# The stores of 48 gate blocks to DRAM, issued by GpSimd instead of ScalarE, in a hybrid decoder trunk

## The chip, the core and the metric

The program runs on one core of one Trainium2 chip. The metric is device time in microseconds (us) of one execution; smaller is better. The engines are named as the profile names them: PE (TensorE), PEld (its weight load), DVE (VectorE), ACT (ScalarE), POOL (GpSimd) and SP (SyncE). ACTq, SPq and POOLq are the instruction queues of these engines where DMAs are issued from them.

## The reference, cut to what matters

Two residual layers (DEPTH 2) on a sequence of 512 rows with 1024 channels, in float32. Each layer projects the normalized input with one matrix, and its columns feed three branches and three blocks of gate logits. The three branch outputs are projected, each is multiplied by the sigmoid of its gate logits, and the sum goes through an output matrix; a gated MLP with a short convolution follows.

```python
h = rmsnorm(x, norm1_g[l])
p = h @ w_in[l]
p_rw, p_ret, p_sg, gate_logits = jnp.split(p, in_cuts, axis=-1)
...
branches = jnp.stack([y_rw, y_ret, y_sg], axis=2)
proj = jnp.einsum('bsgc,gcd->bsgd', branches, w_branch[l])
gates = jax.nn.sigmoid(gate_logits.reshape(B, S, N_BRANCH, D_MODEL))
x = x + jnp.sum(gates * proj, axis=2) @ w_out[l]
x = x + conv_ffn(rmsnorm(x, norm2_g[l]), ffn_w_up[l], ffn_conv_w[l], ffn_conv_b[l], ffn_w_down[l])
```

The gate logits are 3 x 1024 channels, which the kernel holds as 24 blocks of 128 channels by 512 rows for each layer, 48 in all.

## The kernel before, in words

**Matrix products.** Every weight block `wr` comes from DRAM by SP (L136). ACT rounds it to the format fp32r (`wh` or `sh`, L176), DVE subtracts to get the rest (`wl` or `sl`, L181), and PE multiplies in three passes (L198: high by low, high by high, low by high). A weight block is cast two to five blocks ahead of its use. The buffers `wh` and `wl` are three deep, so a cast waits until PE is done with the block three back.

**The gate blocks.** `gates` (L556) is a generator of filler work. While the RWKV branch does its many small and dependent steps, the program takes one step after another from the generator, so that PE always has large matrix products to do. For each of the 24 blocks of a layer PE fills `acc`, DVE multiplies it by the row norm into the tile `gth` (L566), ACT applies tanh in place (L567), and the tile is stored to a block `gd` in DRAM (L569). Much later, in the merge, POOL's queue loads the block back (L1167).

**What else stands on these queues in that stretch.** On ACT: casts of weight blocks, copies `Y`, `GB`, `bk`, `zs`, and in the recurrence (from about 200 us) the copies `U` (L825) and `y` (L842), which PE or DVE then needs. On POOL: masks by affine select (L702, L703), copies of `cs` and `GB` (L899), loads `bkS` (L744), loads of MLP weights `cs` (L337), the small power `rs` for the group norm (L857), loads `yF` (L280), `tab` (L995), and stores `ts` (L308). On SP: weight loads `wr`, the transposing round trips `tr`, `Vt`, `bkS` through DRAM.

**What sets the order.** A scheduler with a timeline of its own puts the instructions of each engine in order when the program is built; each engine then runs its list in that order. Some instructions are pinned to the order in which the code names them. The program also gives each DMA one of a few counters: DMAHW0 to DMAHW7 go round among the DMAs of SP's and ACT's queues, DMASW0 to DMASW7 among those of POOL's queue. A DMA that takes a counter first waits until the DMA before it on that counter has landed. This is seen in the listing with waits, below.

Of the kernel before, what the change touches and what calls it, by code (L numbers as in the profile page):

```python
# [54 lines left out]
class Emit:  # L55
# [500 lines left out]
    def gates(self, l):  # L556
        self.gd = {}
        for br in range(3):
            for m in range(8):
                pg = self.acc()  # L560
                g = self.matFg(pg, ("wall", l, 34 + br * 8 + m, 0), self.h)
                next(g)
                yield
                next(g)
                t = self.u(n="gth")
                self.nc.vector.tensor_tensor(t, pg, self.rsF, op=MUL)  # L566
                self.nc.scalar.activation(t, t, AF.Tanh, scale=0.5)  # L567
                d = self.dp.tile([128, 512], F32, name=self.nm("gd"))
                self.nc.scalar.dma_start(d, t)  # L569
                self.gd[br, m] = d  # L570
                yield

# [1188 lines left out]
```

## Time and profile before

| | us |
|---|---|
| median of 3 runs | 1682.23 (1681.42 to 1682.3) |
| the profiled execution | 1682.15 |
| its span in the profile | 1680.2 |
| PE busy in the span | 1670.6 (99%) |
| DVE busy | 1289.4 (77%) |
| ACT busy | 820.8 (49%) |
| POOL busy | 333.3 (20%) |

The profiled execution is 1.95 us longer than its span, and 0.08 us from the median. The granted TensorE clock is 0.999 over the span. In the timeline a row has the start in us, the duration in us, the engine, the line, the operation with the tile that it writes and what it reads, the count, and in brackets the idle time of the engine before it with what ended it. Rows marked ACTq or SPq are DMA issues, which are not counted as busy; DMA issues of POOL are counted as POOL's work.

### The profile page before, as it was taken

How to read it: one execution, taken by the hardware profiler on the slowest of the kernel's cores; microseconds unless marked ns; L12 is line 12 of the kernel's file. 1: busy time of each engine (PE TensorE's matmuls, PEld its weight loads, DVE VectorE, ACT ScalarE, POOL GpSimd, SP SyncE). 2: the span in 40 equal slices, each digit the busy share in tenths (PEclk: the TensorE clock that was granted, in tenths of full speed). 3: DMA queues.
4: the chain of work that ended last, by engine and by line, in shares of the span. 5: the costliest groups of instructions: out<-in, count | busy, mean ns of one | idle time of the engine just before them, and what ended most of it. 6: DMA issues, size and time to landing. Idle time of an engine off the chain costs nothing.

```text
span 1680.2 us, 29344 instructions
## 1 busy us (share of the span) xinstructions
PE 1670.6 (99%) x10643; PEld 1393.6 (83%) x10643; DVE 1289.4 (77%) x2289; ACT 820.8 (49%) x1436; POOL 333.3 (20%) x514
## 2 busy tenths in 40 slices
PE   9999999999999999999999999999999999999998
PEld 7888877888888888899988888778888888888887
DVE  7788746578668898977868887565785688888897
ACT  6564433554254444456655634435542544444565
POOL 1016013312210111100111260223122012221100
PEclk9999999999999999999999999999999999999999
DMA  5337555644553666668733375646444536665865
GB/s 184 94 102 236 166 180 166 191 129 129 179 191 110 212 216 224 211 226 297 236 111 95 106 227 159 210 155 189 124 141 150 157 128 205 210 203 176 277 232 174
DMA packets 155521, 298.39 MB, mean 178 GB/s; under 512 B 21936, under 2 KB 28848, under 8 KB 155376
## 3 DMA queue, kind: packets, MB, share of 16 engines
q1 hardware_dynamic: 123744, 215.02, 39.9%
q0 software_dynamic: 23280, 66.35, 12.0%
q10 hardware_dynamic: 8352, 15.15, 2.5%
q8 instruction: 83, 1.36, 0.3%
q14 instruction: 62, 0.51, 0.1%
HBM read 236.40 MB, written 60.03 MB: 176 GB/s over the span
## 4 chain that ended last, share of the span: by engine, by line
PE 99%; DVE 1%; DMA 0%; ACT 0%; issue 0%; DVEq 0%; ACTq 0%
PE acc L198 87%; PE sm L198 5%; PE sm L787 2%; PE sm L1044 1%; PE sm L694 1%; PE sm L1155 0%; PE acc L439 0%; PE sm L655 0%; PE sm L656 0%; PE sm L1102 0%; DMA wr<-wall 0%; PE sm L946 0%; PE acc L399 0%; PE sm L937 0%; PE sm L697 0%
## 5 line engine op out<-in xcount | busy, mean ns | idle before, releaser
L198 PE MATMUL acc<-lo,sh 128*128 128x512 f32 (+1 forms) x1144 | 442.6, 387 | 0.0
L198 PE MATMUL acc<-hi,sh 128*128 128x512 f32 (+1 forms) x1144 | 441.6, 386 | 0.0
L198 PE MATMUL acc<-hi,sl 128*128 128x512 f32 (+1 forms) x1144 | 429.3, 386 | 0.1
L176 ACT CAST sh<-wr 128x512 fp32r<-128x512 f32 x352 | 212.3, 616 | 215.3 <-PE acc L198 95.8
L176 ACT CAST wh<-wr 128x512 fp32r<-128x512 f32 x278 | 171.6, 619 | 282.3 <-PE acc L198 214.7
L181 DVE TENSOR_TENSOR wl<-wr,wh 128x512 fp32r<-128x512 f32 x278 | 196.3, 709 | 130.6 <-ACT wh L176 124.2
L181 DVE TENSOR_TENSOR sl<-wr,sh 128x512 fp32r<-128x512 f32 x352 | 238.8, 692 | 70.2 <-ACT sh L176 61.9
L198 PEld LDWEIGHTS acc<-hi,sl 128*128 128x128 f32 x1144 | 214.9, 188 | 44.1 <-DVE sl L181 0.5
L198 PEld LDWEIGHTS acc<-lo,sh 128*128 128x128 f32 x1144 | 215.0, 188 | 43.8 <-issue 0.5
L198 PEld LDWEIGHTS acc<-hi,sh 128*128 128x128 f32 x1144 | 215.0, 188 | 42.6
L198 PE MATMUL acc<-lo,wh 128*128 128x512 f32 (+1 forms) x636 | 244.6, 385 | 0.0
L198 PE MATMUL acc<-hi,wl 128*128 128x512 f32 (+1 forms) x636 | 242.7, 382 | 0.0
L198 PE MATMUL acc<-hi,wh 128*128 128x512 f32 (+1 forms) x636 | 242.4, 381 | 0.0
L1249 ACT ACTIVATE cv<-fu,pc 128x512 f32<-128x512 f32 x88 | 71.8, 816 | 170.1 <-DVE fu L1221 167.2
L198 PEld LDWEIGHTS acc<-hi,wl 128*128 128x128 f32 x636 | 119.6, 188 | 23.9 <-issue 0.7
L198 PEld LDWEIGHTS acc<-lo,wh 128*128 128x128 f32 x636 | 119.6, 188 | 23.3
L198 PEld LDWEIGHTS acc<-hi,wh 128*128 128x128 f32 x636 | 119.7, 188 | 22.3 <-issue 0.2
L1250 DVE SCALAR_TENSOR_TENSOR cv<-fu,pc,cv 128x511 f32<-128x511 f32 x88 | 65.9, 749 | 29.8 <-ACT cv L1249 29.5
L198 PE MATMUL acc<-wl,hi 128*128 128x512 f32 x212 | 85.8, 405 | 0.0
L198 PE MATMUL acc<-wh,lo 128*128 128x512 f32 x212 | 82.5, 389 | 0.0
L198 PE MATMUL acc<-wh,hi 128*128 128x512 f32 x212 | 82.4, 389 | 0.0
L308 POOL DMA_DIRECT2D ts<-pre x60 | 32.5, 542 | 192.1 <-DVE pre L163 184.2
(424 smaller groups left out, 2665.4 us busy)
## 6 DMA issues: line engine op xcount, KB each, us to landing
wr<-wall SPq DMA_DIRECT2D x480, 256.0 KB, 3.0
wr<-ts SPq DMA_DIRECT2D x76, 256.0 KB, 4.3
wr<-wdt SPq DMA_DIRECT2D x66, 256.0 KB, 3.6
pre<-wdt SPq DMA_DIRECT2D x60, 256.0 KB, 3.7
ts<-pre POOLq DMA_DIRECT2D x60, 256.0 KB, 2.7
gd<-gth ACTq DMA_DIRECT2D x48, 256.0 KB, 2.9
gth<-gd POOLq DMA_DIRECT2D x48, 256.0 KB, 3.5
sp<-ab SPq DMA_DIRECT2D x22, 256.0 KB, 5.3
```

The source lines that it names most:

```text
L176: self.at = [self.nc.scalar.copy(hi[:, :n], raw[:, :n])]
L181: self.at.append(self.nc.vector.tensor_tensor(lo[:, :n], raw[:, :n], hi[:, :n], op=SUB))
L198: i = self.nc.tensor.matmul(*x, **y, **kw)
L308: po(self.nc.gpsimd.dma_start(self.tsum[*q, p], t))
L694: i = T.matmul(pK[hv[1 - h], j, :], bk[hv[h], c, 1, :], x[hv[h], c, :], start=True, stop=True)
L787: po(T.matmul(o, l, r, start=start, stop=True, skip_group_check=True))
L1044: po(T.matmul(o, lhsT, rhs, start=start, stop=stop, skip_group_check=True))
L1249: self.nc.scalar.activation(t, u, AF.Identity, scale=self.p("cw2", j), bias=self.p("cb", j))
L1250: V.scalar_tensor_tensor(t[:, 1:], u[:, :511], self.p("cw1", j), t[:, 1:], op0=MUL, op1=ADD)
```

## The change

One word in `gates`: the store of a gate block is issued by `nc.gpsimd` instead of `nc.scalar`. The data, the sizes and all other lines are the same.

```diff
                 self.nc.scalar.activation(t, t, AF.Tanh, scale=0.5)
                 d = self.dp.tile([128, 512], F32, name=self.nm("gd"))
-                self.nc.scalar.dma_start(d, t)
+                self.nc.gpsimd.dma_start(d, t)
                 self.gd[br, m] = d
                 yield
```

The order on PE is the same, row for row. On ACT the 48 store rows are gone and nothing else moves. On POOL 48 rows are added and a few move past each other. On DVE and SP some neighbours swap places.

**ACT in the recurrence of layer 0**, where the copy `U` stands behind a store. Before, with what each row waits for in brackets (PE, DVE and Activation name engines, DMAHW a counter):

```order
L176 CAST wh_2561<-wr_2454 128x512 [waits DMAHW2_49,PE_49]
L176 CAST wh_2619<-wr_2497 128x512 [waits DMAHW4_49,PE_49]
L567 ACTIVATE gth_2577<-gth_2577 128x512 [waits DVE_49]
L569 DMA gd_2580<-gth_2577 128x512 [waits DMAHW2_49,Activation_49]
L825 COPY U_398<-sm_2541 128x256 [waits PE_49]
L176 CAST wh_2683<-wr_2559 128x512 [waits DMAHW5_49,PE_49]
```

Between the tanh of the gate block and the copy `U` stands a store that waits for counter DMAHW2. The change takes that row out, as the difference of the two lists shows:

```order
 L176 CAST wh_2561<-wr_2454 128x512
 L176 CAST wh_2619<-wr_2497 128x512
 L567 ACTIVATE gth_2577<-gth_2577 128x512
-L569 DMA gd_2580<-gth_2577 128x512
 L825 COPY U_398<-sm_2541 128x256
 L176 CAST wh_2683<-wr_2559 128x512
```

The copy `U` now follows the tanh directly.

**SP at the same place, before**, where the counter DMAHW2 was taken last:

```order
L744 DMA bkS_2516<-tr_2518 32x2x128 [waits DMAHW1_49]
L136 DMA wr_2617<-wall 128x512 [waits DMAHW2_49,DVE_49]
L744 DMA bkS_2516<-tr_2518 32x2x128 [waits DMAHW3_49]
L744 DMA bkS_2516<-tr_2518 32x2x128 [waits DMAHW4_49]
L744 DMA bkS_2516<-tr_2518 32x2x128 [waits DMAHW5_49]
```

The weight load `wr_2617` stands between the DMAs on counters 1 and 3; it holds counter 2 when the store on ACT asks for it.

**POOL in the recurrence of layer 0**, where stores now stand ahead of the loads `cs` and of the small power `rs`:

```order
+L569 DMA gd_2475<-gth_2472 128x512
+L569 DMA gd_2580<-gth_2577 128x512
 L337 DMA cs_2653<-wdt 128x512 x2
+L569 DMA gd_2702<-gth_2699 128x512
+L337 DMA cs_2654<-wdt 128x512 x2
 L857 TENSOR_TENSOR rs_522_2668<-s_521_2665,con 128x8
-L280 DMA yF_2671<-tr_2674 32x4x128 x4
-L337 DMA cs_2654<-wdt 128x512 x2
```

The loads `cs_2653` now stand behind the store of the gate block whose tanh precedes `U`; the loads `cs_2654` have moved from behind `yF` to ahead of `rs`, with one store ahead of them. The other layer has the same places.

## The prediction

> **What bounds the kernel now.** I read the page first: the busy shares and the chain that ended last.
>
> ```profile
> span 1680.2 us, 29344 instructions
> ...
> PE 1670.6 (99%) x10643; PEld 1393.6 (83%) x10643; DVE 1289.4 (77%) x2289; ACT 820.8 (49%) x1436; POOL 333.3 (20%) x514
> ...
> PE 99%; DVE 1%; DMA 0%; ACT 0%; issue 0%; DVEq 0%; ACTq 0%
> ```
>
> PE is busy for all but 9.6 us of the span, and the chain is PE from end to end. Its order is the same after the change. So a change on other queues can only take away, or add, time in which PE waits. Which such time there is stands in the list of PE's waits:
>
> ```profile
> PE acc L439 <- DVE rst L436: 1.5, 1, 1.5
> PE sm L787 <- ACT U L825: 1.0, 1, 1.0
> PE sm L787 <- DVE s L849: 0.4, 2, 0.2
> PE sm L694 <- issue: 0.3, 1, 0.3
> ```
>
> 3.2 us in five waits. One of them has to do with ACT, whose queue the change relieves: 1.0 us, once, for the copy `U`. I went to that place in the timeline, on PE, on ACT and on SP:
>
> ```profile
> 216.56 0.39 PE L198 MATMUL acc<-hi,wl 128*128 128x512 f32 x1
> 216.88 0.27 PE L787 MATMUL sm<-U,GB 64*64 64x64 f32 x1
> ...
> 224.97 0.22 PE L787 MATMUL sm<-XB,GB 64*64 64x64 f32 x1
> ...
> 227.72 0.39 PE L198 MATMUL acc<-hi,wl 128*128 128x512 f32 x1
> 229.10 0.27 PE L787 MATMUL sm<-U,GB 64*64 64x64 f32 x1 [0.99 <-ACT U L825]
> ...
> 224.86 0.63 ACT L567 ACTIVATE gth<-gth 128x512 f32<-128x512 f32 x1 [0.33 <-DVE gth L566]
> 228.28 0.35 ACTq L569 DMA_DIRECT2D gd<-gth  x1
> 228.67 0.37 ACT L825 COPY U<-sm 128x256 f32<-128x256 f32 x1 [3.19 <-DMA wr<-wall]
> ...
> 224.71 0.37 SPq L136 DMA_DIRECT2D wr<-wall  x1
> ```
>
> The tanh ends at 225.49, but the store behind it on ACT is issued only at 228.28: 2.79 us in which ACT stands still. The order shows why: the store wants the counter that a weight load of SP holds, and that load was issued at 224.71 and lands some 3.5 us later. `U` stands behind the store and runs at 228.67; PE comes to it right after the matmul at 227.72 and must wait. The same step a round earlier takes 0.32 us (216.56 to 216.88), here 1.38.
>
> **What the change removes.** The store leaves ACT, and `U` follows the tanh. It needs the products of PE that end at 225.19 (the L787 row at 224.97) and ACT, which is free from 225.49 on; its 0.37 us are done at about 225.9, well ahead of 227.72. The step on PE then falls to the 0.32 us of its neighbour: a gain of 1.38 - 0.32 = 1.06 us. Bounds: 0, if something else holds `U`, and 1.06.
>
> The other 47 stores leave ACT too. An issue takes 0.33 us of ACT's queue, 15.7 us for 48, and some wait much longer:
>
> ```profile
> L569 ACTq DMA_DIRECT2D gd<-gth x48: 326/327/369, 99.4 to 1078.5; - x48
> ...
> 210.11 0.63 ACT L567 ACTIVATE gth<-gth 128x512 f32<-128x512 f32 x1 [0.33 <-DVE gth L566]
> 214.22 0.37 ACTq L569 DMA_DIRECT2D gd<-gth  x1
> 214.69 0.62 ACT L176 CAST wh<-wr 128x512 fp32r<-128x512 f32 x1 [3.95 <-DMA bkS<-tr]
> ...
> 973.26 0.63 ACT L567 ACTIVATE gth<-gth 128x512 f32<-128x512 f32 x1 [0.33 <-DVE gth L566]
> 978.11 0.33 ACTq L569 DMA_DIRECT2D gd<-gth  x1
> 978.48 0.62 ACT L176 CAST wh<-wr 128x512 fp32r<-128x512 f32 x1 [4.58 <-DMA wr<-wall]
> ```
>
> Here ACT stood still for 3.48 us (210.74 to 214.22) and for 4.22 us (973.89 to 978.11), with a weight cast behind the store each time. PE's list has no wait for either: the weights are cast ahead, and that cover was longer than 4.2 us. So taking these away gives 0. This is the point at which the large figure, 10.5 us of stalls at three places alone, shrinks to 1.06.
>
> **What the change adds on POOL.** The nearest rows are the stores and loads that POOL issues already:
>
> ```profile
> ts<-pre POOLq DMA_DIRECT2D x60, 256.0 KB, 2.7
> gd<-gth ACTq DMA_DIRECT2D x48, 256.0 KB, 2.9
> ...
> L744 POOL DMA_DIRECT2D bkS<-tr x64: 533/533/728, 150.4 to 1003.7; - x64
> ...
> 159.40 8.50 POOL L744 DMA_DIRECT2D bkS<-tr  x16 [0.34 <-DVE TMP L916]
> ...
> 205.10 2.17 ACT L790 COPY bk<-bkS 128x512 f32<-128x512 f32 x4
> ...
> L1167 POOL DMA_DIRECT2D gth<-gd x48: 536/543/752, 361.7 to 1285.8; - x48
> ...
> 130.00:200.00 70.00, 70.00 (x431) 57.85 (x431) 58.79 (x120) 28.83 (x47) 27.39 (x43) 1.00 0.65 203
> ```
>
> A store of the same size from POOL (`ts`) lands in 2.7 us against 2.9 from ACT, and nobody reads `gd` before 361.7 us; the transfer itself is the same. An issue costs POOL about 0.54 us, bounds 0.53 and 0.75: 48 x 0.54 = 26 us on an engine that is busy for 333 of 1680. I take the middle row because these are DMAs of the same size. The last row is a stretch of 70 us in which most gates of layer 0 are stored (columns PE, PEld, DVE, ACT, POOL): POOL is busy for 27.4 of 70 and would go to about 35.
>
> What counts is who stands behind a store on POOL, since each store waits there for its tanh. The tightest places in layer 0:
>
> ```profile
> 190.60 0.63 ACT L567 ACTIVATE gth<-gth 128x512 f32<-128x512 f32 x1 [0.33 <-DVE gth L566]
> 193.32 2.40 POOL L899 COPY GB<-cs 32x1024 f32<-32x1024 f32 x2 [25.42 <-DVE cs L929]
> 195.67 1.14 POOL L337 DMA_DIRECT2D cs<-wdt  x2
> ...
> 233.61 0.62 ACT L567 ACTIVATE gth<-gth 128x512 f32<-128x512 f32 x1
> 235.22 1.68 POOL L857 TENSOR_TENSOR rs<-s,con 128x8 f32<-128x8 f32 x1 [38.42 <-DVE s L855]
> 236.94 0.69 DVE L859 TENSOR_TENSOR y<-y,rs 128x512 f32<-128x512 f32 x1 [1.87 <-POOL rs L857]
> ...
> 244.85 1.12 POOL L337 DMA_DIRECT2D cs<-wdt  x2
> 249.69 0.69 DVE L163 TENSOR_TENSOR cs<-cs,cs 128x512 f32<-128x512 f32 x1 [4.05 <-DMA cs<-wdt]
> ```
>
> - The copy `GB` (L899) has the store of the gate with the tanh at 190.60 ahead of it: that ends at 191.23, and the issue at 191.8, before 193.32. Cost 0.
> - The power `rs` (L857) now has a store and two `cs` loads ahead. The tanh ends at 234.23, then 3 x 0.54: POOL is free at 235.85 instead of 235.22. `rs` is 0.6 us late, and so is DVE's `y` (L859), on which DVE waits already for 1.87 us. Does PE feel it? The last row answers: DVE stood still for 4.05 us for the `cs` loads, with a weight difference `wl` queued behind, and PE's list has no wait there. 1.87 + 0.6 = 2.5 us stays under that. Cost 0.
> - The first `cs` pair goes from 195.67 to about 229, behind the stores; the second from 244.85 to about 235. Both are wanted by DVE from 245.6 on (249.69 - 4.05) and took about 4 us to come (245.4 to 249.69 for the second). At 239 they are there, and the 4.05 us wait on DVE goes. PE did not feel it, so the gain is 0.
> - The `bkS` loads of layer 0 (rows above) are issued from 150.4 to 167.9; two stores among them make that 1.1 us later, and their reader on ACT comes at 205.10. Cost 0.
>
> In layer 1 the same order meets the same spacing, and PE's list has no wait for `U` there, so there is nothing to gain.
>
> **The sum.** 1682.15 for the profiled execution, of which 1680.2 span and 1.95 around it, minus 1.06: 1681.09. The profiled execution lies 0.08 under the median, so the median after comes to 1681.2. What a measurement of this kernel can tell from no change is about 0.2%, 3.4 us: I forecast no change that shows.
>
> [...]
>
> **The rivals.**
>
> *The stall of `U` stays or comes back elsewhere.* The wait for `U` was a single one of 0.99 us; which round of the recurrence just misses is a matter of a microsecond, and SP's loads now take the counters in another order. Then 1682.2. For it: PE waits twice for DVE's `s` (0.2 us each) in the same stretch, so the margins there are small. Against it: nothing but the tanh is left between PE's products and `U`.
>
> *POOL is late with `rs`, and PE pays.* This ends on the other side. POOL takes its list in order, and a store or load ahead of `rs` that waits for a counter would hold `rs`. DVE waits for it in order, with the next `wl` behind it. It decides from the point at which DVE's wait passes the 4.05 us that were hidden: `rs` more than 2.2 us late (4.05 - 1.87). If a wait of a whole landing (5.7 us, the longest of the `gd` stores, in the row below) fell there, DVE would wait 1.87 + 0.6 + 5.7 = 8.2 us, PE would lose 4.1 in each layer, and the time would be 1681.2 + 8.2 = 1689.4.
>
> ```profile
> DMA to landing us min/median/max: 2.0/3.2/5.7
> ```
>
> Against it: each DMA on POOL waits for the one eight places earlier, and at this place that one is a gate store of the time before 200 us, more than 30 us back.
>
> [...]
>
> *ACT's freed time reaches PE.* If the three stalls were on the path after all, 10.5 us would go: 1671.7. Against it: PE's list has 1.0 us of waits for ACT in all.
>
> *The change does not do what it says.* The stores stand on POOL in the new order, all 48; only if POOL's waits came back to ACT through the `gth` tiles would nothing change. A tile comes round only after several other gate blocks. This falls together with the first rival: 1682.2.
>
> **How the numbers follow.** The forecast, the stall gone and nothing new: 0.68. The stall stays: 0.21. POOL late: 0.06. Locked out: 0.02. ACT's time reaches PE: 0.03. The first two are both within 0.2%: 0.89. Slower by over 0.2%: 0.08; faster: 0.03. The time is 1681.2. The range takes in both likely cases (1681.2 and 1682.2) with the spread of the three runs before (0.9 us) below, and above them 1.4 us for a small loss of the kind of the POOL rival: 1680.2 to 1683.6.
>
> **What would show it.** In the profile after: PE's list without the wait for `U`, and the step from the last matmul to L787 near 227 us at 0.32; the tanh of ACT followed at once by the next instruction, with the idle stretches of 2.8 to 4.2 us gone; no store on ACTq; POOL at about 360 us busy, its stores at 0.54 each; `rs` at about 235.9; the 4.05 us wait of DVE for `cs` gone. The prediction is wrong if PE's waits add up to more than 3.2 us, or if POOL's stores take over 1 us each, or if the time leaves the range with PE's waits unchanged.

## The result, and the profile after

The changed kernel takes 1684.22 us (median of 16 executions, 1682.27 to 1688.81) against 1681.81 before (16 executions on the same chip, 1681.19 to 1682.98). The ratio, which takes in all executions, is 1.0017, with a 95% interval of 1.0009 to 1.0025; by the two medians alone it would be 1.0014. So the change made the kernel 2.4 us slower by the medians, where the prediction had 1681.2 and a range up to 1683.6. A second comparison gave 1.0021 (1.0012 to 1.0030). Two of its twelve executions of the changed kernel, 2380.96 and 2793.79 us at a granted clock of 0.654 and 0.556, are left out of that ratio. The spread is part of the result: 1.8 us before, 6.5 us after.

The page of the changed kernel, its span, its busy times and its chain:

```profile
span 1682.9 us, 29386 instructions
...
PE 1671.8 (99%) x10643; PEld 1394.5 (83%) x10643; DVE 1291.1 (77%) x2289; ACT 819.3 (49%) x1436; POOL 360.2 (21%) x562
...
PE 94%; DVE 2%; DMA 1%; issue 1%; SPq 1%; ACT 0%; POOL 0%; DVEq 0%; POOLq 0%; ACTq 0%
```

The chain is no longer PE from end to end: DVE, DMA and SP's queue stand in it. The list of PE's waits (total, times, longest) says for what:

```profile
PE sm L787 <- DVE S L837: 3.2, 2, 1.7
PE acc L439 <- DVE rst L436: 1.5, 1, 1.5
PE sm L787 <- DVE s L849: 0.4, 2, 0.2
```

The wait for ACT's copy `U` is gone, as predicted. In its place stand two waits for `S`, the state of the recurrence that DVE updates: 1.7 us near 246 us, and 1.4 us at the same place of layer 1. The chain that leads to the first one, in the view that follows it back (start, duration, what), runs over a weight load:

```profile
229.37 4.72 DMA tr<-bkT
...
238.99 0.02 SPq L136
239.01 0.04 issue
239.05 4.52 DMA wr<-wall
...
243.65 0.63 ACT wh L176
244.28 0.02 issue
244.30 0.69 DVE wl L181
244.99 0.34 DVE S L836
245.33 0.02 issue
245.36 0.43 DVE S L837
245.79 0.14 issue
245.93 0.69 PE sm L787 x32
```

A weight block `wr` is issued at 239.05 and needs 4.52 us to land. Only then can ACT cast it (243.65) and DVE subtract (`wl`, 244.30). The update of `S` stands behind that subtraction in DVE's list, so PE gets `S` at 245.9. Before, it looked like this:

```profile
235.37 3.22 SPq L136 DMA_DIRECT2D wr<-wall  x3
...
240.16 0.62 ACT L176 CAST wh<-wr 128x512 fp32r<-128x512 f32 x1 [2.32 <-PE acc L198]
...
242.05 0.43 DVE L837 TENSOR_TENSOR S<-S,F 128x256 f32<-128x256 f32 x1
...
243.86 0.69 PE L787 MATMUL sm<-S,X 64*64 64x64 f32 x32
...
245.97 2.16 POOL L995 DMA_DIRECT2D tab<-rot  x4
```

The same group of weight loads was issued at 235.37, its first block landed 3.8 us later, and the cast at 240.16 waited for PE (2.32 us), not for the load. `S` was done at 242.48, well ahead of its use at 243.86. What is new around it after the change is seen in the timeline of POOL and SP:

```profile
227.10 0.54 POOL L569 DMA_DIRECT2D gd<-gth  x1 [6.60 <-ACT U L825]
227.63 1.10 POOL L337 DMA_DIRECT2D cs<-wdt  x2
234.82 0.55 POOL L569 DMA_DIRECT2D gd<-gth  x1 [6.09 <-ACT gth L567]
235.36 1.09 POOL L337 DMA_DIRECT2D cs<-wdt  x2
236.51 1.69 POOL L857 TENSOR_TENSOR rs<-s,con 128x8 f32<-128x8 f32 x1
238.16 2.20 POOL L995 DMA_DIRECT2D tab<-rot  x4
...
234.23 4.71 SPq L744 DMA_DIRECT2D bkS<-tr  x8
239.05 1.32 SPq L136 DMA_DIRECT2D wr<-wall  x3
```

Three groups of loads of POOL, eight DMAs of 256 KB, have moved: the first pair of `cs` from 195.67 to 227.63, the second from 244.85 to 235.36, and the four loads of `tab` from 245.97 to 238.16, ahead of the loads `yF`. So the second pair and `tab` are in flight just when the weight block is wanted. The windows of 4 us, first before the change, then after it (last two columns: busy share of the DMA engines, GB/s), show it:

```profile
236.00:240.00 4.00, 4.00 (x78) 3.20 (x76) 1.92 (x3) 0.99 (x2) 0.91 (x1) 1.00 0.65 179
240.00:244.00 4.00, 4.00 (x54) 2.88 (x56) 2.05 (x4) 2.97 (x7) 1.39 (x3) 1.00 0.52 181
```

```profile
236.00:240.00 4.00, 4.00 (x78) 3.16 (x77) 2.10 (x3) 0.99 (x2) 3.93 (x6) 1.00 0.87 248
240.00:244.00 4.00, 4.00 (x47) 2.92 (x45) 0.69 (x1) 0.35 (x1) 0.36 (x1) 1.00 0.92 259
```

### The profile page after: what moved, and what is told of

It reads as the page before. It is cut to its first block, busy times and chain, and to the rows that moved or that the text cites. A ratio compares the mean times of both kernels' runs of the same rounds, so it can differ in the third digit from the quotient of the medians.

```text
span 1682.9 us, 29386 instructions
## 1 busy us (share of the span) xinstructions
PE 1671.8 (99%) x10643; PEld 1394.5 (83%) x10643; DVE 1291.1 (77%) x2289; ACT 819.3 (49%) x1436; POOL 360.2 (21%) x562
## 4 chain that ended last, share of the span: by engine, by line
PE 94%; DVE 2%; DMA 1%; issue 1%; SPq 1%; ACT 0%; POOL 0%; DVEq 0%; POOLq 0%; ACTq 0%
PE acc L198 83%; PE sm L198 5%; PE sm L787 2%; PE sm L1044 1%; DMA wr<-wall 1%; PE sm L694 1%; SPq L744 1%; DMA tr<-bkT 1%; PE sm L1155 0%; PE acc L439 0%; PE sm L655 0%; DVE sl L181 0%; PE acc L399 0%; PE sm L1102 0%; PE sm L656 0%
```

## The experiments

Three explanations stood open. **A**: the stores hold POOL's list, and the loads that this moves collide with transfers that PE's next step needs. It has two parts, since the loads moved in two ways: A1, the first pair of `cs`, held until 228 us; A2, the second pair and `tab`, moved forward to 235 to 240 us. **B**: stores through POOL's queue slow other transfers wherever they lie. **C**: SP's own list and its counters, which the change shifts, hold the chain. Each kernel was timed in turn with the kernel before on the same chip.

### Which of the stores

Only the gate blocks up to number 16 of each layer, which lie ahead of the recurrence, on POOL:

```diff
-                self.nc.scalar.dma_start(d, t)
+                (self.nc.gpsimd if 8 * br + m < 17 else self.nc.scalar).dma_start(d, t)
```

> Gate blocks 0 to 16 of each layer (34 of the 48 stores) are issued by GpSimd's queue, the last 7 of each layer, which come within the recurrence, by ScalarE's as before. Theory A (GpSimd's in-order queue: the last stores hold the loads of cs behind them until about 228 us, and the loads then meet the round trip over DRAM and the weight load on the DMA engines): the loads of cs go at about 196 us again, the 1.74 us wait of TensorE for the vector subtraction near 246 us and its twin near 1083 us are gone, the 0.99 us wait for the copy U near 229 us is back; time about that of before, 1681.8. Theory B (any store through GpSimd's queue slows other transfers, wherever it lies): 34 of 48 stores keep about 34/48 of the 3.3 us that the new waits cost, with the 0.99 us wait back: about 1684.1.

Measured: 0.9999 (0.9990 to 1.0008). 34 of the 48 stores on POOL cost nothing. The loads are back at 196.32, 244.95 and 246.07, and PE's list has no wait for `S`. The wait for `U` was not there in layer 0 in this profile; 0.6 us of it stood in layer 1.

The reverse, the last 7 of each layer on POOL and the others on ACT (the same line with the two engines exchanged):

> The reverse: gate blocks 0 to 16 of each layer are stored by ScalarE's queue as before, only the last 7 of each layer (14 of 48 stores) by GpSimd's. Theory A (the in-order queue holds the loads of cs): both new waits of TensorE are there as in the changed kernel (1.7 us near 246, 1.5 us near 1083), the wait for the copy U is gone; about 1684.2. Theory B (every store through GpSimd's queue costs its share): 14 of 48 of 3.3 us, less the 1.06 us of the copy: about 1681.7. Theory C (the order of SP's own instructions and its completion counters, which the change shifts, holds the chain): about 1684 if the counters fall as in the changed kernel, 1681 if not.

Measured: 1.0018 (1.0009 to 1.0027). These 14 stores bring the whole loss. B falls: the number of stores on POOL does not matter, their place does. The profile shows a single new wait, but a longer one, 1.99 us near 245.7; the weight load was issued at 236.55 here and took 6.78 us:

```profile
236.55 6.78 DMA wr<-wall
```

### Holding POOL without moving a store

The stores stay on ACT. POOL copies one column of the gate block, which must wait for the same tanh:

```diff
                 self.nc.scalar.dma_start(d, t)
+                self.nc.gpsimd.tensor_copy(self.small((128, 1), "hold", 2), t[:, 0:1])
```

> The stores stay on ScalarE's queue as before. Instead GpSimd gets, at the place where the changed kernel has a store, a copy of one column of the gate block (128x1), which has to wait for the same tanh: it holds GpSimd's queue as the store does, and moves no store. Theory A (the in-order queue holds the loads of cs): the first pair of cs goes at about 228 us instead of 196, and the waits near 246 and 1083 us are there, 1.5 to 1.8 us each; the wait for the copy U stays too (0.99 us): about 1681.8 + 3.3 = 1685.1. Theory B (the stores' transfers through GpSimd's queue): as before, 1681.8. Theory C (SP's counters): as before, 1681.8.

Measured: 1.0018 (1.0009 to 1.0027), median 1685.89. That is what A expects, but not for its reason. The wait for `S` was 0.31 us and stood in layer 0 alone: here `tab` kept its place behind `yF` (246.61). The rest, some 3 us, came from matmuls far away, which ran slower; the last two experiments go into that. The ratio of this kernel decides nothing.

### Taking the moved loads apart

The changed kernel, with the first pair of `cs` put into the program ahead of the recurrence:

```diff
+        t = [self.rw((128, 2, 512), "cs", 3) for _ in range(2)]
+        self.rs4[3] = RSUM[l, 3], [t[i // 2][:, i % 2, :] for i in range(4)]
+        self.rload(po, *self.rs4[3], (1, 0))
...
-            t = [self.rw((128, 2, 512), "cs", 3) for _ in range(2)]
-            self.rs4[2 * c + at] = q, [t[i // 2][:, i % 2, :] for i in range(4)]
+            if 2 * c + at not in self.rs4:
+                t = [self.rw((128, 2, 512), "cs", 3) for _ in range(2)]
+                self.rs4[2 * c + at] = q, [t[i // 2][:, i % 2, :] for i in range(4)]
...
-            if n == k:
+            if n == k and k != 3:
                 self.rload(po, q, b, (1, 0))
```

> The changed kernel, with one of the two first loads of cs of each layer (the pair at L337) put into the program ahead of the last gate blocks, so that it isn't behind their stores: one pair goes at about 205 us instead of 228. The second pair and the loads of tab stay where the changed kernel has them (235 to 240 us). Theory A1 (the pair at 228 us meets the round trip of tr over DRAM, so that the following weight load is issued late): TensorE's waits near 246 and 1083 us go, the copy U stays without a wait: 1681.8 - 1.06 = about 1680.7. Theory A2 (the second pair and tab, now at 235 to 240 us, meet the weight load itself): the waits stay at 1.5 to 1.8 us, about 1684.2. Both in part: in between, with the round trip of tr at 2.8 us again and the weight load still at 4.5 us.

Measured: 1.0000 (0.9991 to 1.0009). The pair went at 205.39. The wait in layer 1 was gone, that in layer 0 was 1.13 us: in between. The weight load was issued at 236.87, 1.5 us later than in the kernel before, and took 5.65 us. Two of the 11 executions, 1687.71 and 1687.39 us, stand far above the median of 1682.14; they come up again with the clock below.

Of the stores only gate block 21, the one ahead of `U`, on POOL. This holds the first pair alone:

```diff
-                self.nc.scalar.dma_start(d, t)
+                (self.nc.gpsimd if 8 * br + m == 21 else self.nc.scalar).dma_start(d, t)
```

> Of the 48 stores only gate block 21 of each layer (the one ahead of the copy U) is issued by GpSimd's queue, the other 46 by ScalarE's as before. On GpSimd the first pair of cs stands behind this store and so goes at about 227 us, as in the changed kernel; the second pair and the loads of tab keep their places behind the loads of yF, at about 245 us, as before. Theory A1 (the first pair at 228 us slows the round trip of tr, and SP's chain with it): the wait of TensorE near 246 us is there, about 1.7 us, and its twin near 1083 us, 1.5 us: about 1681.8 - 1.06 + 3.3 = 1684. Theory A2 (the second pair and tab, moved to 235 to 240 us, share the DMA engines with the weight load): no such wait, the wait for the copy U gone: 1681.8 - 1.06 = 1680.7, and a narrow spread of the runs.

Measured: 1.0003 (0.9994 to 1.0012). The first pair went at 227.60, the weight load 3 us late at 238.39, and PE has no wait for `S`. So A1 delays SP's chain, as said, but that delay alone fits into the slack. (The delay is not the same each time: with the last stores alone on POOL the first pair went at 227.15 and the weight load only 1.2 us late.)

```profile
227.60 1.10 POOL L337 DMA_DIRECT2D cs<-wdt  x2
...
238.39 1.32 SPq L136 DMA_DIRECT2D wr<-wall  x3
...
241.09 0.62 ACT L176 CAST wh<-wr 128x512 fp32r<-128x512 f32 x1 [2.26 <-DMA wr<-wall]
```

The changed kernel with `tab` kept behind the loads `yF`, by pinning both to the order of the program:

```diff
-            (back or q).dma_start(o[32 * f:32 * f + 32, :] ...)
+            self.tc.keep_in_program_order((back or q).dma_start(o[32 * f:32 * f + 32, :] ...))
...
-            self.nc.gpsimd.dma_start(t[i], self.a["rot"][:, i, c:c + 2, :])
+            self.tc.keep_in_program_order(self.nc.gpsimd.dma_start(t[i], self.a["rot"][:, i, c:c + 2, :]))
```

> The changed kernel, with the loads of tab kept behind the loads of yF on GpSimd's queue (both in program order), so that they go after about 260 us; the two pairs of cs stay at 228 and 235 us, TensorE's, ScalarE's and SP's orders are those of the changed kernel. Theory A1 (the cs pair at 228 us): the waits near 246 and 1083 us stay, about 1684.2. Theory A2 with tab as the larger part of it (two thirds of the 1.5 MB that moved to 235 to 240 us): the waits shrink to under 0.7 us each, about 1681.5, with few runs above 1684.

Measured: 0.9998 (0.9989 to 1.0006), and a spread of 2.3 us. The lists of PE, ACT and SP are those of the changed kernel, so C falls: the loss goes when four loads of POOL move, with SP's list untouched. The wait in layer 0 was 0.87 us, a little over the 0.7 expected; that in layer 1 was gone.

Both edits together:

> The changed kernel with both edits: the first pair of cs ahead of the last gate blocks (about 205 us) and the loads of tab behind those of yF; only the second pair of cs stays at 235 us. Theories A1 and A2 alike: the waits near 246 and 1083 us are gone or under 0.4 us, the wait for the copy U as well: 1681.8 - 1.06 = about 1680.7, faster than both kernels by 0.06% and 0.2%, the runs no wider than those of before (some 3 us). If neither theory holds (the waits come from SP's own order and counters): they stay, 1684.

Measured: 0.9997 (0.9988 to 1.0005), median 1681.76 against 1682.55 of the kernel before. No wait for `S` and none for `U` is left in PE's list. Against the changed kernel the loss is undone. Against the kernel before, the gain of 1 us that was expected is not told from nothing.

The changed kernel again, beside these three:

> The changed kernel once more, on the chip of the other three, as their measure: about 1.0017 of before, its waits near 246 and 1083 us at 1 to 2 us, and its times spread over 6 us. Where the granted clock of an execution is 0.997 to 0.998, its time is 3 to 5 us above the others, if a wait of about 2 us lowers TensorE's clock for some microseconds after it (as the profile of the kernel with the last stores alone on GpSimd showed: clock 0.5 from 246 to 250 us, behind a wait of 2.0 us).

Measured: 1.0021 (1.0012 to 1.0030). The wait was 1.44 us in layer 0, and none in layer 1 this time. Of the ten executions in the ratio three had a granted clock of 0.998 or less: 1685.29, 1685.97 and 1691.20 us, against 1683.00 to 1685.95 of the other seven. So one of the three stands clear, and the 3 to 5 us that I expected for each were not there. The granted clock is taken up below.

Then the order alone, with no store moved: the kernel before, with the second pair and `tab` ahead of the first loads `yF`. Not shown in the diff are the set-up of `self.late` and the loads of `tab`, which are pinned to the order of the program as above.

```diff
-        for f in range(4):
-            (back or q).dma_start(...)
+        def load():
+            for f in range(4):
+                self.tc.keep_in_program_order((back or q).dma_start(...))
+        if back is None or self.late != []:
+            return load()
+        self.late.append(load)
...
-            if i in (3, 5):
-                tabs.append(self.tabs(l, i - 3))
+            if i in (0, 1):
+                tabs.append(self.tabs(l, 2 * i))
+                if i == 1:
+                    self.late.pop()()
+                    self.late = None
```

> The kernel before, all stores on ScalarE, with the second pair of cs and the loads of tab put ahead of the first loads of yF on GpSimd's queue, where the changed kernel has them (the loads of yF wait until those of tab are in the program): they go at about 237 to 240 us instead of 245 to 248. Theory A2 (these loads share the DMA engines with the weight load): TensorE waits near 244 us without any store having moved; the weight load is issued at 235.4 here, 1.2 us ahead of where the kernel with the last stores alone on GpSimd had it (wait 2.0 us), so 0.5 to 1.5 us, 1.0003 to 1.0012 of before. If the stores on GpSimd's queue are needed: no wait there, 1.0000.

Measured: 1.0003 (0.9994 to 1.0012), and no wait for `S`. This is a miss of my expectation, and it sharpens A2. The loads went at 237.44 and 238.57, about as late as in the changed kernel, but the weight load had gone ahead of them:

```profile
235.95 3.21 SPq L136 DMA_DIRECT2D wr<-wall  x3
...
237.44 1.14 POOL L341 DMA_DIRECT2D cs<-wdt  x2
238.57 2.12 POOL L1003 DMA_DIRECT2D tab<-rot  x4
...
240.73 0.62 ACT L176 CAST wh<-wr 128x512 fp32r<-128x512 f32 x1 [2.32 <-PE acc L198]
```

Side by side, for layer 0 (start of each group in us, and when the first block of the group of weight loads landed; the wait of PE for `S` in the profiled execution):

| | first `cs` | second `cs` | `tab` | weight load | landed | wait | ratio |
|---|---|---|---|---|---|---|---|
| before | 195.7 | 244.9 | 246.0 | 235.4 | 239.2 | 0 | 1 |
| changed | 227.6 | 235.4 | 238.2 | 239.1 | 243.6 | 1.74 | 1.0017 |
| changed, again | 226.5 | 234.2 | 237.0 | 237.5 | 242.1 | 1.44 | 1.0021 |
| early stores only | 196.3 | 245.0 | 246.1 | 234.6 | 240.1 | 0 | 0.9999 |
| last stores only | 227.2 | 234.9 | 237.7 | 236.6 | 243.3 | 1.99 | 1.0018 |
| holding, no store | 226.9 | 234.5 | behind `yF` | 238.4 | 241.5 | 0.31 | 1.0018 (slower matmuls) |
| first pair early | 205.4 | 234.9 | 237.7 | 236.9 | 242.5 | 1.13 | 1.0000 |
| one store | 227.6 | behind `yF` | behind `yF` | 238.4 | 241.0 | 0 | 1.0003 |
| `tab` late | 227.2 | 234.9 | behind `yF` | 238.6 | 242.2 | 0.87 | 0.9998 |
| both | 205.3 | 234.9 | behind `yF` | 236.4 | 241.1 | 0 | 0.9997 |
| order alone | 196.2 | 237.4 | 238.6 | 236.0 | 240.6 | 0 | 1.0003 |

The column "landed" decides. A block that landed by 241.1 us cost nothing, and each that landed from 241.5 on made PE wait. Wherever PE waits, its step on `S` starts 2.36 or 2.37 us after the landing, in every one of these profiles: the time of the cast, the subtraction and the two updates of `S`, with the handing on between them.

Two things move the landing: when the load is issued, and how long it takes. Issued at 238.4 to 239.1 us it took 2.6 us with neither the second pair nor `tab` issued ahead of it (one store), 3.1 and 3.7 with the second pair (holding, `tab` late) and 4.5 with both (changed). Issued at 236.4 to 236.9 it took 4.7 us with the second pair (both edits), and 5.6 and 6.8 with `tab` as well. What else makes a load long is not separated here: with the early stores only it took 5.5 us with none of these loads near, but was issued at 234.6 and landed in time.

Each wait of over 0.5 us has the second pair issued ahead of the weight load, and something more: `tab` within 2 us of it, or the weight load itself late by 3 us. The second pair alone (both edits) or the late weight load alone (one store) stays within the slack; `tab` alone was not tried that close.

### What a longer wait does to the clock

The executions of the changed kernel differ in a second number, the granted TensorE clock over the whole span. In the first 16, the five at 0.998 or less took 1686.22 to 1688.81 us, the other eleven 1683.46 on average. Of the 83 executions of the kernel before that were timed beside the kernels above none was that low (one of 20 later, at 1686.64), and none of the 44 of the kernels with early stores only, one store, `tab` late and both. The two long executions of the kernel with the first pair early were that low, and so were three of 11 with the last stores on POOL. The profile of that last kernel happened to hold such an execution; no such execution of the changed kernel itself was profiled. In windows of 1 us (PEclk is the third column from the right):

```profile
244.00:245.00 1.00, 0.00 (x0) 0.00 (x0) 0.94 (x2) 1.00 (x4) 0.00 (x0) 1.00 1.02 385
245.00:246.00 1.00, 0.31 (x12) 0.34 (x16) 0.51 (x2) 0.96 (x4) 0.00 (x0) 0.86 0.72 275
246.00:247.00 1.00, 1.00 (x33) 0.88 (x26) 0.09 (x1) 0.88 (x2) 0.00 (x0) 0.50 0.78 268
...
248.00:249.00 1.00, 1.00 (x3) 0.76 (x3) 0.97 (x2) 0.00 (x0) 0.58 (x2) 0.50 0.32 53
249.00:250.00 1.00, 1.00 (x5) 0.79 (x4) 0.27 (x1) 0.00 (x0) 1.00 (x2) 0.94 0.71 236
```

Behind the wait of 1.99 us the clock is at half for 3.4 us (from 245.72 to 249.12 by the shares 0.86 and 0.94). To tell whether the wait does that, I made the wait by itself: the kernel before, with k operations S = max(S, S) on DVE behind the update of `S` at that place (k of 6, 8, 10 and 12).

```diff
-                    po(V.tensor_tensor(St, St, f, op=MUL))
+                    po(V.tensor_tensor(St, St, f, op=MUL)); [po(V.tensor_tensor(St, St, St, op=MAX)) for _ in range(6 if l == 0 and c == 2 else 0)]
```

> The kernel before, with 6 more vector operations (S = max(S, S), which leave S as it is) behind the update of S in the third round of the first layer, where the changed kernel's first new wait lies. One is 0.45 us by the distance of the two updates of S (242.05 after 241.60 us); S was 1.33 us early there (done at 242.48, used at 243.86, 0.05 us of passing on): TensorE waits 6 x 0.45 - 1.33 = 1.4 us. Theory D (a wait of about 2 us or more lowers TensorE's granted clock for some microseconds): below that point, so 1.4 us and no more, about 1.0008 of before, granted clock as before, the spread of the runs that of before (3 us). Theory E (the long executions of the changed kernel have another cause, such as weight loads that now and then land later): the same here.

> 8 of these operations: a wait of 8 x 0.45 - 1.33 = 2.3 us. Theory D: at or just over the point, so that some or all executions pay 1.3 to 3 us more for the lowered clock: 1.0014 to 1.003, runs 4 to 6 us apart, the long ones at a granted clock of 0.998 or lower. Theory E: 2.3 us and no more, 1.0014, clock as before.

> 10 of these operations: a wait of 10 x 0.45 - 1.33 = 3.2 us. Theory D: every execution pays the lowered clock, so 3.2 us and 1.3 to 5 us besides: 1.0027 to 1.005, granted clock 0.998 or lower in all of them, and 0.5 in the profile for some microseconds behind the wait. Theory E: 3.2 us and no more, 1.0019, clock as before.

> 12 of these operations: a wait of 12 x 0.45 - 1.33 = 4.1 us. Theory D: 4.1 us and 1.3 to 5 us besides, 1.0032 to 1.0055, the clock lowered for at least as long as with 10. Theory E: 4.1 us and no more, 1.0024, clock as before.

| operations | wait in the profile | clock at half, us | ratio | executions at 0.998 or less |
|---|---|---|---|---|
| 6 | 1.93 | none | 1.0016 (1.0006 to 1.0025) | 3 of 10 |
| 8 | 2.85 | 6.8 | 1.0029 (1.0017 to 1.0041) | 5 of 6 |
| 10 | 3.8 | 3.4 | 1.0030 (1.0019 to 1.0041) | 8 of 8 |
| 12 | 4.7 | 6.8 | 1.0037 (1.0024 to 1.0050) | 4 of 5 |

Each wait is about 0.55 us longer than expected, because one `wl` of 0.69 us runs among the operations. So the kernel with 6 operations met neither theory's 1.4 us and 1.0008. With 8 operations the view of 1 us shows the half clock again:

```profile
245.00:246.00 1.00, 0.00 (x0) 0.00 (x0) 0.97 (x3) 0.00 (x0) 1.00 (x2) 0.91 0.55 172
246.00:247.00 1.00, 0.29 (x12) 0.32 (x15) 0.53 (x2) 0.00 (x0) 1.00 (x3) 0.50 0.99 115
...
251.00:252.00 1.00, 1.00 (x4) 0.81 (x3) 0.00 (x0) 0.00 (x0) 0.54 (x1) 0.50 1.03 402
252.00:253.00 1.00, 1.00 (x7) 0.48 (x6) 0.00 (x0) 0.00 (x0) 0.00 (x0) 0.68 0.94 377
```

The wait began at about 243.9. The half clock began at 245.82, still within the wait, and ended at 252.64. The medians rise by 5.5, 6.0 and 7.5 us for 8, 10 and 12 operations, 2.2 to 2.8 us more than the profiled wait. So the wait lowers the clock: theory D of the expectations holds, and E, another cause of the long executions, is not needed. By length alone the point lies near 2 us: in the profiles 1.74 and 1.93 us left the clock full, 1.99 us did not, and with 6 operations it went either way.

The windows and the traces show more. The half clock lasts 3.40 us with the last stores alone on POOL and with 10 operations, and 6.82 us with 8 and 12 operations (by the shares of the windows of 1 us): one or two times 3.41 us. The traces of the kernel before and of the changed kernel list the granted clock with its times. In both, a half clock comes 1672.531 us after the first entry, at the end of the run, although the first entry lies at 4.91 us of the span in one and at 7.62 us in the other. From these figures I estimate that the changes of the clock lie on a grid with cells of about 3.41 us, which starts with the first entry. In the 3.41 us ahead of the half clock PE waited for 1.99 us with the last stores alone, for 1.96 us with 8 operations, for 3.27 us with 10 and for all 3.41 us with 12. In the changed kernel, on this grid, the wait of 1.74 us lay within one cell, and the clock stayed full. Between 1.74 and 1.96 us in one cell no profile tells: of the 1.93 us with 6 operations no view shows how they lay in the cells. The first entry of the two traces differs by 2.7 us; if the grid lies elsewhere in each execution, that fits the mixed outcome with 6 operations.

### The slower matmuls of the holding kernel

Between 452 and 488 us, far from any held store, the holding kernel had 156 matmuls of 128x512, the kernel before 160. The narrow target tile was the first suspect, so the hold was repeated with tiles of 16 columns:

```diff
-                self.nc.gpsimd.tensor_copy(self.small((128, 1), "hold", 2), t[:, 0:1])
+                self.nc.gpsimd.tensor_copy(self.small((128, 16), "hold", 2)[:, 0:1], t[:, 0:1])
```

> The holding copies on GpSimd once more (stores on ScalarE, loads of tab behind those of yF, both pairs of cs held to about 227 and 235 us), the same program but for the target tile of the copy: 16 columns (64 bytes of a partition) instead of 1 (4 bytes), since the profile with 1 column showed 128x512 matmuls far from any hold at 233 ns instead of 227 ns, 3 us in all. If these 3 us came from where the narrow tile pushed the other tiles: the matmuls are at 227 ns again, and what is left is the hold of the cs pairs alone, 0 to 0.4 us at 244 us: 1681.8 to 1682.5, ratio 0.9997 to 1.0004. If the slowness of the holding kernel came from the hold: 1.0018 again.

Measured: 1.0042 (1.0029 to 1.0056), 1690.5 us: worse, not better, so a tile of 64 bytes is no remedy. Its wait for `S` was 0.86 us, with the pairs of `cs` held to 226.61 and 234.24 and no store moved, about that of the kernel with `tab` late (0.87); the weight load was issued at 238.61 and landed at 241.78. That much of A needs no store on POOL.

Then the tiles without the holds: the kernel before, with two copies into the same two tiles at the first gate block.

> The kernel before with the same two 64-byte target tiles that the second holding kernel had, but only two copies into them, at the first gate block; no other hold, no store moved. If the slower matmuls of the holding kernels (233 instead of 227 ns, 8 us with the 64-byte tiles) come from where these tiles push the small tiles behind them: about 1690, ratio 1.004, and about 156 matmuls of 128x512 in the 36 us from 452 to 488 us instead of 160. If they come from the 48 copies on GpSimd: as before, 1.000, 160 matmuls.

Measured: 1.0043 (1.0027 to 1.0060), 1690.48 us, with no wait of PE that the kernel before lacks. The matmuls of two stretches, first before, then with the two tiles (busy and count of PE, then of PEld):

```profile
452.00:488.00 36.00, 36.00 (x160) 29.81 (x159) 1.00 0.54 183
1280.00:1320.00 40.00, 40.00 (x178) 33.14 (x177) 1.00 0.44 145
```

```profile
452.00:488.00 36.00, 36.00 (x156) 28.98 (x155) 1.00 0.53 179
1280.00:1320.00 40.00, 40.00 (x173) 32.20 (x172) 1.00 0.46 145
```

So the two tiles do it, with two copies instead of 48, and the holding does not. Why tiles of 128 bytes of a partition in all slow matmuls at a full granted clock stays open.

## Why the prediction was wrong

**What bounds the kernel**: right. PE sets the time, and the change acts only through PE's waits.

**The gain at `U`**: right in its mechanism, sized too firmly. In the changed kernel `U` follows the tanh (226.71 behind 226.17), and PE goes from the matmul at 229.04 to L787 at 229.35, the predicted 0.32. But the 1.06 us came from one execution, and what ended that wait was a weight load's landing. Ten profiles of kernels that keep this store on ACT show 0 to 2.1 us of waits for `U`, 0.7 us on average (0 in five of them). This is the step "a gain of 1.38 - 0.32", which I took for a constant.

**ACT's other stalls, 10.5 us for nothing**: right. They are gone from ACT, and no time came back with them.

**POOL's issues**: right. 0.54 us each, POOL busy for 360.2 us where about 360 was predicted, `rs` at 236.51 where 235.9 was. No run shows POOL locked out, for which 0.02 was set aside: the longest issue of the 48 stores took it 0.73 us, with DVE busy for 77% of the span. The stores took a median of 3.3 us to land, not the 2.7 of `ts`; PE's list has no wait for them. The rival that priced POOL's lateness by `rs` looked at the wrong reader.

**The loads that trade places**: this is the step that failed. It reads: "The first `cs` pair goes from 195.67 to about 229, behind the stores; the second from 244.85 to about 235 ... so the gain is 0." Both times were right to 2 us. But I asked only whether their own reader gets them in time, and DVE did: its 4.05 us wait is gone. I did not ask which transfers they would now meet, and I did not count the four `tab` loads at all, which moved with them. Eight DMAs of 256 KB went into 227 to 240 us, where the next weight block was to come. The term should have been: that weight block 3.7 us later in issue (239.05 for 235.37) and 4.5 us in landing (3.8 before), against a slack that ran out; two waits, 1.7 and 1.4 us, and more where the clock fell. PE's waits came to 5.1 us, above the 3.2 that the prediction named as a sign of being wrong. By the medians the loss is 2.4 us; by the mean of the changed kernel's eleven executions at 0.999 or more it is 1.5 (1683.46 - 1681.92, the mean of the 16 before).

**The range**: its upper end, 1.4 us above the second case, was a guess for small losses at `rs`. The loss had another place, and a step in it, the half clock behind a wait of PE, that no row of the profile before could show. (The lower end, 1681.2 - 0.9, is 1680.3, not 1680.2; it decides nothing.)

Between the two profiled executions the span grew by 2.7 us. That is not the effect in small: 1.3 us of it stood in the first 8 us, as the last section tells, and the second profile of the changed kernel has a span of 1681.3.

## What to carry to other kernels

When an edit puts an instruction that waits into a list that runs in order, follow every DMA behind it to its new time, and ask not only whether its reader is served but which other transfer it now meets; the reader to watch is the next weight block, not the moved data. A wait that a transfer's landing ends is a draw, not a constant (0 to 2.1 us for `U` in ten profiles): look at more than one execution before it becomes a term of a sum. A wait of TensorE near 2 us or more can cost more than its length: behind 1.99 us and more the clock was at half for 3.4 or 6.8 us in these profiles, and with waits of 2.85 to 4.7 us the medians rose by 2.2 to 2.8 us more than the wait.

## What had not been expected of the hardware

- The half clock behind waits of about 2 us: 1.99 us of wait and 3.4 us of half clock in one profile, 2.85 and 6.8 in another. By the estimate above the changes of the clock lie on a grid of about 3.41 us; a wait of 1.93 us left the clock full in its profile.
- Slow matmuls at the start, for a time that differs from execution to execution. In windows of 2 us, the matmuls of the kernel before and then of the changed kernel:

```profile
6.00:8.00 2.00, 2.00 (x11) 1.61 (x10) 1.12 (x3) 1.78 (x3) 0.00 (x0) 1.00 1.05 394
```

```profile
6.00:8.00 2.00, 2.00 (x7) 1.57 (x6) 0.99 (x3) 1.61 (x3) 0.00 (x0) 1.00 1.05 400
```

  7 instead of 11 matmuls in the same 2 us, although the clock column reads 1.00; in the second profile of the changed kernel there are 11 again. The column misleads here: the first entry of a granted clock in the trace, a full one, comes at 4.91 us before and at 7.62 us after, and ahead of it the 1.00 stands for no entry. There the large matmuls start 0.427 us apart, later about 0.227. Up to 1.3 us between executions come from here.
- Two small tiles that nothing needs cost 8 us: 1690.48 us against 1682.78, with 156 instead of 160 matmuls in 36 us at a full granted clock. The cause is open.
